# A decoder layer on one core: its mixers' second half earlier, operands in halves, and low parts of weights on another engine

## The chip, the cores and the metric

The kernel runs on one core of one Trainium2 chip. The metric is the device time of one execution in microseconds (us), the median of several runs. Engines are named as in the profile: PE (TensorE, matrix products), DVE (VectorE), ACT (ScalarE), POOL (GpSimd) and SP (SyncE, which issues most transfers).

## What is computed

One layer on 1024 positions of width 1024, all in float32. Two token mixers in parallel (a causal gMLP in 8 groups with chunks of 128, and a latent attention of 16 heads), then cross-attention into 256 memory tokens, then a mixture of experts: 8 groups of 8 experts, the best group, two experts in it, each of width 256.

```python
def hybrid_layer(x, mem, positions, ...):
    proj = x @ w_in + b_in
    u, v, c_q, c_kv, k_rope_raw, gate_gm, gate_mla = jnp.split(proj, IN_SPLITS, axis=-1)
    y_gm = gmlp_branch(gelu(u), gelu(v), gm_ln_g, gm_ln_b, gm_w_s, gm_b_s) @ w_gm_out
    y_mla = mla_branch(c_q, c_kv, k_rope_raw, positions, ...) @ w_mla_out
    merged = sigmoid(gate_gm) * y_gm + sigmoid(gate_mla) * y_mla
    x = layer_norm(DEEPNORM_ALPHA * x + merged @ w_o, ln1_g, ln1_b)
    x = layer_norm(DEEPNORM_ALPHA * x + memory_cross_attention(x, mem, ...), ln2_g, ln2_b)
    y_moe = hierarchical_moe(x, ...)
    return layer_norm(DEEPNORM_ALPHA * x + y_moe, ln3_g, ln3_b)
```

The gMLP branch is `u * (tril(w_s) @ layer_norm(v) + b_s)` by chunks and groups; an expert is `(silu(x @ w_gate) * (x @ w_up)) @ w_down`.

## The kernel before

Every float32 product is made of three: each operand is split into a rounded high part (ACT copies it into the type float32r) and a low part (the difference, a subtraction, mostly on DVE), and `mm3` (L123) adds high by high, high by low and low by high. `split` (L108) makes both parts, `load_w` (L114) loads a weight tile and splits it. Raw weight tiles have three buffers, split ones five, so loads and splits run several projections ahead of PE.

The dense stages (all up to the router) aren't ordered by hand: a planner orders the instructions of each engine and the issues of SP by its own model of time, keeping data and buffer dependencies. From the router on, in `manual_schedule` regions, PE, ACT, DVE and POOL run in the order in which the program emits them (the first `turn_x` of the experts lies between two such regions); SP's issues are still the planner's.

The stages in order:

- `latents` (L220): x is loaded transposed in 8 tiles of 512 KB (`xraw`) with a weight tile (`w_cq`) for every two, split, and multiplied as it comes. `late_consts` (L205) then makes the router's constants and loads six small ones (`b_t`, `g_q`, `g_kv`, `b_s`, `rope_c`, `b_r`); the first reader is the scaling of the latent (L264).
- `mla_proj`, `proj_v`: queries, keys and values of the attention go to DRAM; so does v of the gMLP.
- Gates and gMLP: `proj_in_t` (L311) makes one block of 128 columns, 48 products of 512 columns. Projections 8 to 23 alternate with the 8 steps `st` of each half of `gmlp` (L674). The call `gmlp(half)` loads four v tiles, normalizes and splits them into `vs` (one buffer), and each step writes its block of the result to `a_d` in DRAM.
- `load_a` (L737) loads `a_d` back in 8 tiles of 512 KB (`aT`) and splits them. Then come the last projection from `xT`, the pools of the attention (`mla_pools`; they reuse the memory of `xT`) and `gate_gm` (L744), whose 8 projections alternate with steps of `mla`: the first step loads q, k and v of head 0 (`load`, L478), the second runs the first product with them (L506).
- `mla`: attention by hand, in one list. The sums of the softmax go to DRAM and come back as `fac` in a chain of small transfers issued by POOL (`factors`, L762).
- `mem_kv` (L634): key projections f = 0 to 7 of the memory (24 products of 256 columns each), then value projections. Between them `scale_o` (L789) scales the attention output, one block a step: two products of `fac` with a selection (L798), then DVE.
- `merge`, `out_ln`, `mem_attn`, `out_ln`, then the router.
- The experts: 32 pairs. Each pair has six weight tiles of 1 MB (four of gate and up, two of down); tile m is `raw`, then `high(m)` on ACT (`wh`), then `low` (`wl`, L1435). `ahead` in `experts` (L1447) prepares one tile ahead at each of six points of a pair; `low(m)` also issues the load of tile m + 11 or m + 12. Tiles with m % 6 == 5 (`slow`) get their low part on POOL, the others on DVE. `turn_x` (L1312) transposes a pair's gathered rows and splits them, `hidden` (L1335) applies Silu and the mask, `store` (L1390) adds up the output.
- Before the first pair, `router_masks` (L1162) sums the masks on PE and DVE, `warm` (L1155) puts products without a reader on PE, and tiles 0 to 2 get their parts: the low parts of 0 and 1 on DVE, that of 2 on POOL.
- `final_loads` (L1557) spreads the last norm's two vectors over 128 partitions with products in full float32, in pairs 20 to 24; `final` (L1573) adds, normalizes and stores 8 row tiles.

## Time and profile before

| | us |
|---|---|
| median of 3 runs | 2033.64 (2032.84 to 2034.22) |
| profiled execution | 2035.97 |
| its span, first to last instruction | 2034.2 |
| PE busy | 1977.6 (97%) |
| DVE busy | 1292.5 (64%) |
| ACT busy | 1003.3 (49%) |
| POOL busy | 449.2 (22%) |

[...] The page's 40 slices show PE at nine tenths or more in all but three: the first, the one around 1400 and the last. How to read it: PE is the engine with the least idle time, so another engine's time matters only where PE waits for it.

### The profile page before, as it was taken

To read this page: it belongs to the slowest core of one execution; us is meant where nothing else is said; L and a number is where in the kernel's file an instruction comes from. 1 tells how busy PE (TensorE), PEld (TensorE's weight loads), DVE (VectorE), ACT (ScalarE), POOL (GpSimd) and SP (SyncE) were. 2 spreads that over 40 slices of the span, in tenths; PEclk is the share of its full clock that TensorE was granted. 3 is DMA by queue.
4 is the path that set the end of the run, shared out by engine and by line. 5 is a ranking of instruction groups with operands and counts; after the bars stand their busy time and mean duration, and the time that the engine had idled before them with its cause. 6 is when DMAs were issued, how large, how long until landed. Compare 5 with 4: busy or idle time off the path is not lost.

```text
span 2034.2 us, 25602 instructions
## 1 busy us (share of the span) xinstructions
PE 1977.6 (97%) x9468; PEld 1630.4 (80%) x9468; DVE 1292.5 (64%) x2040; ACT 1003.3 (49%) x1267; POOL 449.2 (22%) x243
## 2 busy tenths in 40 slices
PE   8999999999999999999999999997999999999996
PEld 8888888888787777777888888886788888888884
DVE  5636533441335888857436516477888888888887
ACT  4432422322304777764212315233777777777774
POOL 0002000000100111110001100022545555557752
PEclk9999999999999999999999999997999999999998
DMA  5154963353783555537535712555899999999966
GB/s 184 54 210 155 382 196 134 143 189 136 245 251 104 126 125 125 125 133 239 184 106 180 268 62 73 161 218 231 286 372 381 381 387 396 401 392 369 377 260 250
DMA packets 147897, 457.29 MB, mean 225 GB/s; under 512 B 18077, under 2 KB 64029, under 8 KB 118744
## 3 DMA queue, kind: packets, MB, share of 16 engines
q1 hardware_dynamic: 138040, 438.58, 61.7%
q0 software_dynamic: 9728, 17.03, 2.2%
q8 instruction: 76, 1.25, 0.2%
q14 instruction: 53, 0.43, 0.1%
HBM read 367.10 MB, written 104.79 MB: 232 GB/s over the span
## 4 chain that ended last, share of the span: by engine, by line
PE 91%; DMA 3%; DVE 3%; ACT 1%; issue 1%; SPq 0%; POOL 0%; POOLq 0%; ACTq 0%
PE bank L125 9%; PE bank L126 9%; PE bank L127 9%; PE py L1355 8%; PE bank L380 8%; PE bank L382 8%; PE bank L384 8%; PE pg L125 6%; PE pg L127 5%; PE pg L126 5%; PE po L564 2%; PE po L566 2%; PE po L565 2%; PE st L538 1%; PE st L540 1%; PE st L542 1%
## 5 line engine op out<-in xcount | busy, mean ns | idle before, releaser
L1426 ACT ACTIVATE wh<-raw 128x2048 fp32r<-128x2048 f32 (+1 forms) x198 | 361.1, 1859 | 36.3 <-issue 31.4
L1435 DVE TENSOR_TENSOR wl<-raw,wh 128x2048 fp32r<-128x2048 f32 (+1 forms) x166 | 363.3, 2236 | 4.6 <-PE pg L126 3.0
L1435 POOL TENSOR_TENSOR wl<-raw,wh 128x2048 fp32r<-128x2048 f32 x32 | 202.9, 6340 | 227.6 <-ACT wh L1426 227.6
L110 ACT ACTIVATE wsp<-wraw 128x1024 fp32r<-128x1024 f32 (+5 forms) x118 | 111.6, 947 | 263.7 <-PE bank L384 155.2
L125 PE MATMUL pg<-wh,ex 128*128 128x512 f32 x512 | 203.4, 397 | 0.7 <-ACT ex L110 0.7
L126 PE MATMUL pg<-wl,ex 128*128 128x512 f32 x512 | 200.0, 391 | 2.0 <-DVE wl L1435 2.0
L127 PE MATMUL pg<-wh,ex 128*128 128x512 f32 x512 | 200.6, 392 | 0.0
L111 DVE TENSOR_TENSOR wsp<-wraw,wsp 128x1024 fp32r<-128x1024 f32 (+5 forms) x118 | 127.6, 1083 | 96.2 <-ACT wsp L110 93.7
L1355 PE MATMUL py<-wh,ehs 128*128 128x512 f32 x512 | 143.7, 402 | 2.9 <-DVE ehs L111 2.4
L380 PE MATMUL bank<-xT,wsp 128*128 128x512 f32 x384 | 120.1, 390 | 0.0
L382 PE MATMUL bank<-xT,wsp 128*128 128x512 f32 x384 | 119.9, 390 | 0.0
L384 PE MATMUL bank<-xT,wsp 128*128 128x512 f32 x384 | 119.7, 390 | 0.0
L735 POOL TENSOR_TENSOR xr<-xr,lb 128x1024 f32<-128x1024 f32 x12 | 28.7, 2395 | 409.4 <-ACT xr L734 409.4
L546 ACT ACTIVATE pe<-st 128x768 f32<-128x768 f32 (+5 forms) x128 | 86.3, 674 | 59.6 <-DVE st L544 59.5
L126 PEld LDWEIGHTS pg<-wl,ex 128*128 128x128 f32 x512 | 96.7, 189 | 21.3 <-DVE wl L1435 2.3
L125 PEld LDWEIGHTS pg<-wh,ex 128*128 128x128 f32 x512 | 96.4, 188 | 21.1 <-ACT lgb L1571 1.5
L127 PEld LDWEIGHTS pg<-wh,ex 128*128 128x128 f32 x512 | 96.5, 189 | 20.6
L1355 PEld LDWEIGHTS py<-wh,ehs 128*128 128x128 f32 x512 | 91.3, 189 | 19.4 <-DVE ehs L111 3.1
L125 PE MATMUL bank<-wsp,xT 128*128 128x512 f32 (+2 forms) x256 | 91.2, 363 | 6.5 <-ACT wsp L110 6.5
L319 ACT ACTIVATE to<-bank,cols 128x512 f32<-128x512 f32 x48 | 30.4, 684 | 133.7 <-PE bank L384 133.7
L548 ACT ACTIVATE pq<-pe 128x768 fp32r<-128x768 f32 (+5 forms) x128 | 91.3, 713 | 4.1
L126 PE MATMUL bank<-wsp,xT 128*128 128x512 f32 (+2 forms) x256 | 91.6, 358 | 0.0
(410 smaller groups left out, 4627.4 us busy)
## 6 DMA issues: line engine op xcount, KB each, us to landing
raw<-w_gu SPq DMA_DIRECT2D x124, 1024.0 KB
raw<-w_dn SPq DMA_DIRECT2D x62, 1024.0 KB
wraw<-w_t SPq DMA_DIRECT2D x24, 512.0 KB
kn_d<-st SPq DMA_DIRECT2D x8, 1024.0 KB
qn_d<-st SPq DMA_DIRECT2D x8, 1024.0 KB
vv_d<-vt SPq DMA_DIRECT2D x16, 512.0 KB
qT<-qn_d SPq DMA_DIRECT2D x16, 512.0 KB
kT<-kn_d SPq DMA_DIRECT2D x16, 512.0 KB
```

What stands on the lines that cost most here:

```text
L110: a = nc.scalar.activation(hi, src, AF.Copy)
L111: (lo_eng or nc.vector).tensor_tensor(lo, src, hi.bitcast(F32), op=ALU.subtract)
L125: mm(out, ah, bh, start=start, stop=False)
L126: mm(out, ah, bl, start=False, stop=False)
L127: mm(out, al, bh, start=False, stop=stop)
L380: mm(ps, wh, x.at(0, kt, h), start=st, stop=False)
L382: mm(ps, wh, x.at(1, kt, h), start=False, stop=False)
L384: mm(ps, wl, x.at(0, kt, h), start=False, stop=sp)
L548: nc.scalar.activation(pq[:, 0, q0:], e[:, q0:], AF.Copy)
L1355: self.nc.tensor.matmul(py[:, q * 512:(q + 1) * 512], hs[:, a, js], w[b][:, j * 1024 + q * 512:j * 1024 + (q + 1) * 512], start=start and ...
L1426: self.nc.scalar.activation(w[0][:, c], self.raws[n][:, c], AF.Copy)
L1435: eng.tensor_tensor(w[1][:, c], self.raws[n][:, c], w[0][:, c].bitcast(F32), op=ALU.subtract)
```

## The change

- Start: the first x tile and the first weight tile are loaded and split in two halves each, alternating, x first. The six small constants are issued by POOL instead of SP, each made to wait for the rounding of the last x tile.
- Mixers: `gmlp(1)` stands before projection 15 instead of after it, its steps go with projections 17 to 20 instead of 18 to 21, and `load_a` has two projections (22, 23) behind it instead of one.
- `mem_kv`: the first step of `scale_o` that stands between key projections comes after f = 6 instead of f = 5.
- Experts: the low part of tile 0 goes to DVE between the two halves of the mask products, that of tile 1 after the masks, then the first pair's rows are transposed and split, then the low part of tile 2, on DVE instead of POOL. A Silu of one column stands behind the `warm` products on ACT. Tile 5's low part is DVE's too (`slow` from m = 11 on).
- Final vectors: four row halves, each loaded, split into high and low and spread by two float32r products, one half every two pairs from 20 to 28, instead of float32 products on whole rows.
- Tail: the last row tile's last operation and its store are done in halves.

```diff
--- before.py
+++ after.py
@@ -202,10 +202,12 @@
         self.ones = p.tile([128, 128], FR, name="ones")
         ts(self.ones, jp, 0.0, 1.0, op0=ALU.mult, op1=ALU.add)
 
-    def late_consts(self):
+    def late_consts(self, behind):
+
         self.router_consts()
         for t, n in ((self.bt, "b_t"), (self.gq, "g_q"), (self.gkv, "g_kv"), (self.bs, "b_s"), (self.fr, "rope_c"), (self.rb, "b_r")):
-            self.nc.sync.dma_start(t, self.i[n])
+            d = self.nc.gpsimd.dma_start(t, self.i[n])
+            self.tc.add_manual_dep(d.ins, behind.ins.name, mybir.DependencyInfo(mybir.DependencyClass.Sync, mybir.DependencyReason.DATA), reason="behind larger transfers")
 
     def natural(self, ps, t, x, w, kts=range(8), nk=8):
 
@@ -227,8 +229,20 @@
             for kk in range(4):
                 for kt in (2 * kk, 2 * kk + 1):
                     raw = self.gp.tile([128, 1024], F32, name="xraw", tag="g")
+                    if kt == 0:
+
+                        wraw = self.rawp.tile([128, 1024], F32, name="wraw", tag="wraw")
+                        wt = self.wp.tile([128, 2, 1024], FR, name="wsp", tag="wsp")
+                        cs = [(slice(512 * j, 512 * j + 512), slice(384 * j, 384 * j + 384)) for j in range(2)]
+                        for c, cw in cs:
+                            nc.sync.dma_start(raw[:, c], self.i["xT"][kt][:, c])
+                            nc.sync.dma_start(wraw[:, cw], self.i["w_cq"][kk][:, cw])
+                        for c, cw in cs:
+                            self.split(xT.at(0, kt, c), xT.at(1, kt, c), raw[:, c])
+                            self.split(wt[:, 0, cw], wt[:, 1, cw], wraw[:, cw])
+                        continue
                     nc.sync.dma_start(raw, self.i["xT"][kt])
-                    self.split(xT.at(0, kt, ALL), xT.at(1, kt, ALL), raw)
+                    self.last = self.split(xT.at(0, kt, ALL), xT.at(1, kt, ALL), raw)
                     if kt % 2 == 0:
                         wt = self.load_w(self.i["w_cq"][kk], 768)
                 for kt in (2 * kk, 2 * kk + 1):
@@ -236,7 +250,7 @@
                     for t in range(8):
                         self.natural(pss[t][:, :384], t, xT, lambda k: (wt[:, 0, o:o + 384], wt[:, 1, o:o + 384]), [kt])
                     self.unit()
-            self.late_consts()
+            self.late_consts(self.last)
             bcq = small.tile([128, 384], F32, name="bcq", bufs=1)
             self.bcast(bcq, self.i["b_cq"])
             bkv = small.tile([128, 320], F32, name="bkv", bufs=1)
@@ -654,7 +668,7 @@
             self.load_o(f)
             if f == 0:
                 next(fac, None)
-            if f in (5, 7):
+            if f in (6, 7):
                 next(scale)
         for sl in range(2):
             wts = [self.load_w(self.i["w_mv"][sl, kk], 1024) for kk in range(4)]
@@ -1444,11 +1458,10 @@
         gi = self.main[0]
         return {i: self.gather(i, gi[:, i:i + 1]) for i in range(3)}
 
-    def experts(self, rest, xg):
+    def experts(self, rest, xg, x):
         nc, tc = self.nc, self.tc
         gi, si, al = self.main
-        xs = {}
-        xs[0] = self.turn_x(xg[0], 2)
+        xs = {0: x}
         mask = self.main_mask
         ready = 0
         order = contextlib.ExitStack()
@@ -1457,7 +1470,7 @@
         for i in range(NP):
             def ahead():
                 nonlocal ready
-                slow = lambda m: m % 6 == 5 and m < 6 * NP - 6
+                slow = lambda m: m % 6 == 5 and 6 < m < 6 * NP - 6
                 m = ready + 2
                 self.high(m + 1)
                 if slow(m + 1):
@@ -1491,7 +1504,7 @@
                 sel = self.select(gi[:, NP - 1:])
             if i == 24:
                 self.nb = nc.values_load(self.nbi[0:1, 0:1], min_val=0, max_val=15)
-            if i in (22, 24):
+            if 21 <= i <= 28:
                 next(lgb, None)
             if i == NP - 1:
                 self.flush()
@@ -1558,16 +1571,18 @@
         nc = self.nc
         self.lgb = px.enter_context(self.pool("lgb", side="right")).tile([128, 2, 1024], F32, name="lgb")
         self.fin = px.enter_context(self.pool("fins", 8, side="right"))
-        one = self.fin.tile([1, 128], F32, name="one", bufs=1)
-        nc.gpsimd.memset(one, 1.0)
         for j, n in enumerate(("ln3_g", "ln3_b")):
-            row = self.fin.tile([1, 1024], F32, name="row", bufs=1)
-            nc.sync.dma_start(row, self.i[n])
-            yield
             for q in range(2):
                 c = slice(q * 512, (q + 1) * 512)
+                high, low = (self.fin.tile([1, 512], FR, name=m, bufs=1) for m in ("high", "low"))
+                row = self.lgb[:1, j, c]
+                nc.sync.dma_start(row, self.i[n][:, c])
+                yield
+                self.split(high, low, row)
+                yield
                 pg = self.bank_g()
-                nc.tensor.matmul(pg, one, row[:, c], start=True, stop=True)
+                nc.tensor.matmul(pg, self.ones[:1], high, start=True, stop=False)
+                nc.tensor.matmul(pg, self.ones[:1], low, start=False, stop=True)
                 nc.scalar.activation(self.lgb[:, j, c], pg, AF.Copy)
 
     def final(self, first=True):
@@ -1620,8 +1635,12 @@
                 nc.scalar.activation(u, u, AF.Copy, scale=r)
                 nc.gpsimd.tensor_tensor(u, u, lb, op=ALU.add)
             else:
-                stt(u, u, r, lb, op0=ALU.mult, op1=ALU.add)
-            nc.sync.dma_start(self.out[t], u)
+                for c in halves if t == 7 else [slice(0, 1024)]:
+                    stt(u[:, c], u[:, c], r, lb[:, c], op0=ALU.mult, op1=ALU.add)
+                    if t == 7:
+                        nc.sync.dma_start(self.out[t][:, c], u[:, c])
+            if t < 7:
+                nc.sync.dma_start(self.out[t], u)
 
         rows = [row_sum(t) for t in range(8)]
         for t in range(9):
@@ -1707,20 +1726,20 @@
                             st(2 * j)
                             k.proj_in_t(xT, 11 + j)
                             st(2 * j + 1)
+                        st = k.gmlp(1)
                         k.proj_in_t(xT, 15)
-                        st = k.gmlp(1)
                         k.proj_in_t(xT, 16)
-                        k.proj_in_t(xT, 17)
                         for j in range(4):
                             st(2 * j)
-                            k.proj_in_t(xT, 18 + j)
+                            k.proj_in_t(xT, 17 + j)
                             st(2 * j + 1)
-                        k.proj_in_t(xT, 22)
+                        k.proj_in_t(xT, 21)
                         k.flush()
-                    w = k.load_w(k.i["w_t"][23], 1024)
+                    w = k.load_w(k.i["w_t"][22], 1024)
                     aT = Act(front.enter_context(k.pool("aT", 8, side="right")), "aT")
                     k.load_a(aT)
-                    k.proj_in_t(xT, 23, w)
+                    k.proj_in_t(xT, 22, w)
+                    k.proj_in_t(xT, 23)
                     k.flush()
                 k.mem_load(late)
                 k.mla_pools(mla)
@@ -1796,15 +1815,17 @@
                 wts.remove(q)
     m = k.router_masks()
     next(m)
+    k.low(0, nc.vector)
     k.warm(6)
     next(m, None)
     k.warm(16)
+    nc.scalar.activation(k.rp.tile([128, 1], F32, name="silu"), k.i128[:, :1], AF.Silu)
     k.high(2)
-    for n in range(2):
-        k.low(n, nc.vector)
-    k.low(2, nc.gpsimd)
+    k.low(1, nc.vector)
+    x = k.turn_x(xg[0], 2)
+    k.low(2, nc.vector)
     order.close()
-    k.experts(rest, xg)
+    k.experts(rest, xg, x)
     return k
 
 
```

## Rows read from the trace of the kernel before

**Rows 1.** Page, part 1: engine, busy us (share of the span), instructions.
```profile
PE 1977.6 (97%) x9468; PEld 1630.4 (80%) x9468; DVE 1292.5 (64%) x2040; ACT 1003.3 (49%) x1267; POOL 449.2 (22%) x243
```

**Rows 2.** Timeline, start: start, us, engine line operation tiles [idle before, releaser].
```profile
6.53 2.93 PE L125 MATMUL bank<-wsp,xT 128*128 128x384 f32 x8 [6.53 <-ACT wsp L110]
...
6.89 1.06 ACT L110 ACTIVATE xT<-xraw 128x1024 fp32r<-128x1024 f32 x1 [0.41 <-DMA xraw<-xT]
...
22.87 1.06 ACT L110 ACTIVATE xT<-xraw 128x1024 fp32r<-128x1024 f32 x1 [0.29 <-DMA xraw<-xT]
...
50.02 1.84 ACT L264 ACTIVATE cqT<-bank,cols 128x512 fp32r<-128x512 f32 x3 [3.12 <-PE bank L262]
```

**Rows 3.** Chain that ended last, its first piece: start, us, what.
```profile
0.77 3.89 DMA xraw<-xT
```

**Rows 4.** Timeline, end of the mixers: SP's issues, then PE.
```profile
529.17 3.83 SPq L741 DMA_DIRECT2D aT<-a_d  x8
...
541.17 0.47 SPq L489 DMA_DIRECT2D kT<-kn_d  x1
...
552.98 0.76 PE L506 MATMUL bank<-kT,qT 96*128 96x256 f32 x2 [4.41 <-DMA kT<-kn_d]
...
553.55 1.05 PE L380 MATMUL bank<-aT,wsp 128*128 128x512 f32 x2
...
558.37 0.62 PE L380 MATMUL bank<-aT,wsp 128*128 128x512 f32 x2
```

**Rows 5.** Chain that ended last: down products, final vectors' products.
```profile
1792.11 4.11 PE py L1355 x18
...
1813.95 1.91 PE pg L1570 x4
```

**Rows 6.** Waits of PE, whole span: us in total, times, longest.
```profile
PE py L1355 <- DVE ehs L111: 2.4, 1, 2.4
...
PE bank L382 <- DVE aT L111: 0.6, 1, 0.6
```

**Rows 7.** Timeline, scaling of the attention output, PE.
```profile
919.77 1.21 PE L798 MATMUL bank<-fac,fsel 32*128 32x512 f32 x2 [2.26 <-DMA fac<-rinv_d]
```

**Rows 8.** Stretches: us, PE PEld DVE ACT POOL busy, PEclk, DMA, GB/s.
```profile
910.00:915.00 5.00, 5.00 (x44) 5.00 (x43) 2.74 (x4) 1.28 (x3) 0.52 (x1) 1.00 1.02 374
...
920.00:925.00 5.00, 5.00 (x21) 4.35 (x22) 3.56 (x5) 1.46 (x2) 0.00 (x0) 0.50 0.93 299
```

**Rows 9.** Timeline, pairs 2 and 5: low parts on DVE and POOL.
```profile
1464.22 6.34 DVE L1435 TENSOR_TENSOR wl<-raw,wh 128x2048 fp32r<-128x2048 f32 x1
...
1519.97 2.28 DVE L1435 TENSOR_TENSOR wl<-raw,wh 128x2048 fp32r<-128x2048 f32 x1
...
1520.30 6.44 POOL L1435 TENSOR_TENSOR wl<-raw,wh 128x2048 fp32r<-128x2048 f32 x1 [7.79 <-ACT wh L1426]
```

**Rows 10.** Timeline, start of the experts: POOL, DVE, PE, ACT.
```profile
1408.24 4.56 POOL L1435 TENSOR_TENSOR wl<-raw,wh 128x2048 fp32r<-128x2048 f32 x1 [0.22 <-ACT wh L1426]
...
1408.49 0.23 DVE L1170 COPY pws<-pov 128x64 f32<-128x64 f32 x1 [1.81 <-PE pov L1168]
...
1408.75 4.09 DVE L1171 TENSOR_TENSOR pws<-pws 128x32 f32<-128x32 f32 x1
...
1411.61 0.60 PE L1317 MATMUL px<-ident,xg 128*128 128x128 f32 x4
...
1418.20 1.11 PE L1317 MATMUL px<-ident,xg 128*128 128x128 f32 x4 [2.01 <-DVE ex L111]
...
1424.75 1.28 ACT L1339 ACT_TABLE_LOAD   x1
...
1430.99 1.03 PE L1317 MATMUL px<-ident,xg 128*128 128x128 f32 x8
```

**Rows 11.** Waits of DVE, 1800 to 1960: us in total, times, longest.
```profile
DVE eh L1340 <- ACT eh L1339: 16.2, 12, 1.5
```

**Rows 12.** Chain that ended last, its last piece.
```profile
2027.71 1.29 DVE raw L1623
```


## The prediction, on record before the changed kernel was run

> **What bounds the kernel now.** I read the busy table of the page first: PE is busy for 97% of the span [rows 1]. So only three things can move the time: time in which PE waits, time in which it runs at the lower of its two clocks, and products that it need not do. The second view was the list of what PE waited for, and the third the table by stretches, read for the granted clock. The span holds 56.6 us in which PE isn't busy, and nearly all of them lie in a handful of places: the start, the end of the mixers, the scaling of the attention output, the start of the experts, and the tail. From pair 3 of the experts on, PE waits for nothing until the last pair. The fourth view was the timeline around each place, engine by engine, to see which instruction came last there. Each part of the change goes to one of these places, so I price them one by one and add.
>
> **The start.** PE's first product comes at 6.53 [rows 2]. Ahead of it in one chain stand the landing of the first x tile (512 KB, 3.89 us from issue) [rows 3], its rounding on ACT (1.06, as that of the next tile [rows 2]) and that of the weights (the rest, 6.53 - 4.66 - 1.06 = 0.8). Now x and weights come in halves, x half first. The next x tile is rounded from 6.89 on, after a wait for its landing [rows 2]; so 384 KB of weights and 512 KB of x landed in the 2.2 us since 4.66, or 0.41 MB per us. A half tile of 256 KB is then there some 0.6 us before the whole, at about 4.05 (estimate). Half a rounding of x is about 0.6, half of one of weights about 0.5 (both estimates a little over the half, for an instruction's start): first product at 5.2, a gain of 1.3. PE isn't starved behind it, since the products of one x tile take it longer than the next tile's landing. Bounds: 1.6, and a loss of 0.3 if the halves land one behind the other rather than together. [...]
>
> The six small constants leave SP's queue for POOL's and wait there for the rounding of the last x tile, which ended at 23.9 in the trace [rows 2]. POOL has nothing queued behind them until the projections of the attention. Their first reader is the scaling of the latent at 50.02 [rows 2], so there are 26 us for six small transfers: nothing gained, nothing lost. If that cover were gone, the loss would be what they come late.
>
> **The mixers.** The second half of the gMLP stands one projection earlier, and two projections, not one, stand between the loads of its result (aT) and its first use. In the trace SP issues the eight aT loads (4 MB) from 529.17 on; one projection later the tiles of head 0 reuse xT's memory, and kT is issued at 541.17 behind them. It lands 11.7 us later, and PE waits 4.41 for it [rows 4]. What follows runs slow: the two products with kT and twelve of the next projection take from 552.98 to 558.37 [rows 4], 5.4 us, where twelve at 0.228 each [rows 5] and two half as wide take 3.0: 2.4 lost. PE also waited 0.6 for aT's low part [rows 6]. Sum 7.4. With two projections (some 22 us) behind the load, aT's 4 MB are through (10 us at 0.41 MB per us) before head 0 is issued. Ahead of kT then stand about 2 MB, 5 us and a latency, against the 11 us of the projection that hides it (48 products at 0.228): the wait goes, and nothing is late next. Moved with it: the setup of the second half (four v tiles, DVE and ACT work) must be ready one projection sooner; it has the same two projections of cover as the first half has, for which PE didn't wait. Bounds 0 and 7.6; I take 7.4.
>
> **The scaling.** One step of it moves behind the seventh key projection instead of the sixth. PE waited 2.26 for fac [rows 7]; in the next 5 us it did 21 products at a granted clock of 0.50, against 44 in 5 us before it at 1.00 [rows 8]. Two of the 21 are twice as wide, so they count as 23, or 2.6 us at full clock: 2.4 lost. The key projection that now stands in between has 24 products, 2.7 us at 44 in 5 us, which covers the 2.26 with 0.5 to spare. Gain 2.26 + 2.4 = 4.7; bounds 0 (fac later by as much as it is hidden) and 5.0.
>
> **The start of the experts.** Three low parts (2.28 us each [rows 9]) matter here. The third ran on POOL from 1408.24; DVE's add of 32 columns for the masks, issued at 1408.75, took 4.09 [rows 10]. The same happens at 1464.22, a low part of 6.34 on DVE [rows 9]. So an operation on DVE with two operands in SBUF waits while POOL's runs. Behind the add stood both other low parts and the low half of x, so PE's second four transposes came at 1418.20, although the first four ran at 1411.61 [rows 10]. Now the first low part fills DVE's wait of 1.81 ahead of the copy of the masks [rows 10], so the copy comes 0.45 later, the add costs 0.2 and not 4.09, the second low part ends at about 1412.0, the low half of the first half of x (after its rounding on ACT) at 1413.5, and the transposes follow to 1414.1 (if they again wait for that half). The 48 products of the pair at 0.228 [rows 5] and 0.2 of turning the hidden rows end at 1425.3, against 1430.99 [rows 10]: 5.7. The table load of 1.28 for Silu, in the trace after the first products [rows 10], falls into ACT's idle time before. Taken off again: the third and sixth low part are now DVE's. Six low parts are 13.7 us; with some 4.4 us of small work DVE has 18.1 in a pair that takes PE 17.7. I take off 0.7: 5.0. Bounds: 1 (DVE gives the rest back in the next two pairs) and 6. The wait of 2.4 in the third pair [rows 6] I leave as it is.
>
> **The final vectors.** Four products of full float take 1.91 us, twice [rows 5]; they become eight rounded ones at 0.228, 1.8 in all. Gain 3.8 - 1.8 = 2.0; bounds 0 and 2.5. The four new splits (some 0.6 each on ACT and DVE) stand at the head of four pairs; DVE waits up to 1.5 for ACT before the gate of a pair (16.2 in 12 waits [rows 11]), which covers them. Their rows are four small loads on SP, each a whole pair ahead of its split.
>
> **The tail.** The last multiply-add takes 1.29 and ends the work [rows 12]; the store of 512 KB follows. In halves, the second store is 256 KB: 0.6 less at 0.41 MB per us, the first being under way. Bounds -0.3 and 0.8. [...]
>
> **Sum.** 1.3 + 7.4 + 4.7 + 5.0 + 2.0 + 0.6 = 21.0. The profiled execution took 2035.97 and would take 2015.0. It lay 2.33 above the median of the runs, 2033.64, which becomes 2012.6. The median is what I predict.
>
> **The rivals.** (a) The plan of the first stages isn't fixed by hand, so the new order may leave a wait where kT's was: head 0's loads still wait for xT's memory, and only 3 us are spare. Then most of the 7.4 stays, say 5.5: 2018. For it speaks that kT took 11.7; against it that the 4 MB ahead of it are gone. (b) DVE becomes the bound in the first pairs, and 4.5 of the 5.0 come back as waits for low parts: 2017. For it speaks the wait of 2.4 in pair 2, behind a DVE that was late; against it that DVE has some 2.6 us to spare in each later pair. (c) fac is again late, its chain of small transfers being slowed by others: 2017.3. (d) Slower: POOL keeps every sixth low part from the second pair on. In the steady pairs DVE's low part starts only 0.33 before POOL's (1519.97 against 1520.30) [rows 9]. If DVE comes later by more than that, it is POOL that starts first, DVE is held 4.1 (6.34 less 2.28 [rows 9]), and PE waits 2.4 [rows 6]. Lost in all 30 pairs, that is 72, less the one already there: 2082. The work that the change puts on DVE pushes this way. [...] Against it speaks that the trace lost the order once, in pair 2, and had it back from pair 3 on: PE's wait gives DVE the time. (e) The change doesn't do what it says, because the planner puts loads and steps where they were: then only the last three parts are left, and where DVE gives those back as well, 2031.
>
> **How the numbers follow.** Forecast, all six parts within their small errors: 0.52, with a range of its own of 2009 to 2016. (a) 0.13, (b) 0.14, (c) 0.07, two of these together (2021 to 2023) 0.06, (e) 0.04, (d) 0.04. The likeliest is the forecast, 2012.6. The range runs from 2009 (the upper bounds of the parts add up to 2.5, and pair 2 may lose half its wait) to 2021, which takes in (a), (b) and (c) alone, and leaves out 0.14 with the pairs of rivals, (d) and (e). About 0.2%, 4 us, is what a measurement of this kernel can tell from no change. Faster by more: 0.92; within: 0.04, which is (e); slower: 0.04, which is (d).
>
> **What would show it.** Right: PE's first product near 5.2; no wait for kT and none for fac, and a granted clock of 1.00 in both stretches; the masks' add at 0.2 us, and the second four transposes of x before 1415 on the old clock; eight short products for the vectors. Wrong: a new wait of more than 2 us in PE's list, above all one for a low part in the first three pairs, or DVE low parts above 6 us in more than one pair.

## The result: 17.5 us faster, 3.9 behind the forecast

| | before | after |
|---|---|---|
| median | 2033.93 (4 runs, 2032.84 to 2035.64) | 2016.47 (4 runs, 2015.20 to 2018.18) |
| ratio | | 0.9914, 95% interval 0.9897 to 0.9931 |
| profiled execution | 2035.97 | 2016.14 |
| its span | 2034.2 | 2014.4 |

The forecast was 2012.6 with a range of 2009 to 2021. The time lies inside it, on the slow side. PE does the same number of products and waits less; its busy time falls too (against [rows 1]), mostly because products at the lower clock count as busy for longer (in [rows 8], 21, two of them of double width, fill 5.00 us at 0.50 and 44 at 1.00; the clock records of both traces hold only these two values) and fewer of them run at it (mean granted clock 0.989 against 0.985). First part 1 of the page of the changed kernel, then its list of what PE waited for (us in total, times, longest), cut to the lines that answer to [rows 4, 6, 7] and one new one:

```profile
PE 1969.8 (98%) x9468; PEld 1624.5 (81%) x9468; DVE 1293.0 (64%) x2049; ACT 1006.0 (50%) x1274; POOL 462.1 (23%) x246
```
```profile
PE py L1369 <- DVE ehs L111: 2.4, 1, 2.4
PE pm L520 <- DMA kT<-kn_d: 1.9, 5, 0.6
...
PE bank L520 <- issue: 1.4, 1, 1.4
```

The wait for fac is gone, that for aT too. The 2.4 for ehs in the third pair is still there, as said. Of the 4.41 for kT a wait of 1.4 is left at the same product, with no releaser named.

Where the time went shows best as a **lead**: the start of the same product in both traces, before minus after.

| product | before | after | lead | gained since the line above | forecast |
|---|---|---|---|---|---|
| first of all | 6.53 | 4.95 | 1.58 | 1.6 | 1.3 |
| first with cqT | 163.80 | 161.53 | 2.27 | 0.7 | 0 |
| first with kT | 552.98 | 546.75 | 6.23 | 4.0 | mixers, |
| last with aT | 634.95 | 626.36 | 8.59 | 2.4 | 7.4 together |
| first key projection of the memory | 897.83 | 889.46 | 8.37 | -0.2 | 0 |
| last with fac | 955.86 | 941.62 | 14.24 | 5.9 | 4.7 |
| first transposes of the experts | 1411.61 | 1397.82 | 13.79 | -0.4 | 0 |
| transposes in the first pair, for the second | 1430.99 | 1411.12 | 19.87 | 6.1 | experts' start, |
| the same for the fifth | 1487.99 | 1469.74 | 18.25 | -1.6 | 5.0 together |
| the same for the last | 1971.08 | 1952.05 | 19.03 | 0.8 | 2.0 |
| end of the span | 2034.2 | 2014.4 | 19.8 | 0.8 | 0.6 |

The parts gave 19.8 where 21.0 was forecast. The places themselves, in the timeline of the changed kernel (start, us, engine line operation tiles) and in the tables by stretch (us, PE PEld DVE ACT POOL busy, PEclk, DMA share, GB/s).

**Start**, answering to [rows 2, 3]. Timeline of the changed kernel; then stretches of the kernel before, from 6 and 12, and of the changed one, from 5 and 9:

```profile
4.95 1.65 PE L125 MATMUL bank<-wsp,xT 128*128 128x384 f32 x4 [4.95 <-ACT wsp L110]
6.39 0.52 PE L126 MATMUL bank<-wsp,xT 128*128 128x384 f32 x1
6.71 0.52 PE L127 MATMUL bank<-wsp,xT 128*128 128x384 f32 x1
```
```profile
6.00:10.00 4.00, 3.47 (x11) 3.47 (x12) 3.87 (x4) 3.33 (x4) 0.00 (x0) 1.00 1.02 405
12.00:16.00 4.00, 4.00 (x25) 4.00 (x24) 2.85 (x3) 1.35 (x3) 0.24 (x1) 1.00 0.63 172
```
```profile
5.00:9.00 4.00, 4.00 (x13) 4.00 (x14) 1.83 (x4) 1.11 (x2) 0.00 (x0) 1.00 0.80 303
9.00:13.00 4.00, 4.00 (x25) 4.00 (x24) 2.86 (x3) 3.40 (x4) 0.00 (x0) 1.00 1.03 415
```

The first products of the program start 0.32 apart, later ones 0.17. In 4 us PE does 11 (in the 3.47 that were left) or 13 of them, and then 25: half the rate, though PEclk shows 1.00, so it is the spacing that has to be read here. (The first clock record of the trace lies at 11.9 before and at 8.8 now, just where the spacing changes; ahead of it the table counts 1.00 for want of a record.) The slow beginning lasted from 6.53 to 11.82 before, 16 products, and from 4.95 to 8.88 now, 12 products. That difference isn't the halves' doing: in the eleven kernels below that start in the same way it is 9 to 19 products. From the first product to the 31st it takes 7.1 here, 6.7 to 8.1 in those eleven, and 7.7 in the kernel before.

**Mixers and scaling**, answering to [rows 4, 7, 8]. Changed kernel: SP's issues and PE's first product with kT, the stretch behind that and the one in front of it, and the first product with fac, which has no wait now; last, a stretch of the kernel before that follows the second one of [rows 8]:

```profile
515.99 4.28 SPq L755 DMA_DIRECT2D aT<-a_d  x8
...
537.27 1.16 SPq L503 DMA_DIRECT2D kT<-kn_d  x1
...
546.75 0.48 PE L520 MATMUL bank<-kT,qT 96*128 96x256 f32 x2 [1.36 <-issue]
```
```profile
540.00:547.00 7.00, 5.64 (x26) 4.41 (x25) 1.29 (x2) 1.06 (x1) 0.00 (x0) 1.00 1.09 263
547.00:552.00 5.00, 5.00 (x24) 4.16 (x24) 1.85 (x6) 0.00 (x0) 0.00 (x0) 1.00 1.07 310
```
```profile
911.40 0.73 PE L812 MATMUL bank<-fac,fsel 32*128 32x512 f32 x2
```
```profile
925.00:930.00 5.00, 5.00 (x33) 4.51 (x32) 1.97 (x4) 1.82 (x4) 0.00 (x0) 0.84 0.23 89
```

Behind the 1.36 at 546.75 the clock stays at 1.00 (24 products in 5 us), so the low stretch of the kernel before is gone. The 1.36 itself isn't fixed: at the same product the eleven kernels below with the new order of the mixers have 0.2 to 2.95. In the kernel before, the low clock behind the wait for fac went on past 925: 0.84 in the mean of the next 5 us.

**Start of the experts**, answering to [rows 10]: DVE, then PE:

```profile
1392.59 2.29 DVE L1449 TENSOR_TENSOR wl<-raw,wh 128x2048 fp32r<-128x2048 f32 x1
1394.79 0.22 DVE L1184 COPY pws<-pov 128x64 f32<-128x64 f32 x1
1395.05 0.19 DVE L1185 TENSOR_TENSOR pws<-pws 128x32 f32<-128x32 f32 x1
...
1397.82 0.70 PE L1331 MATMUL px<-ident,xg 128*128 128x128 f32 x4
...
1399.92 0.66 PE L1331 MATMUL px<-ident,xg 128*128 128x128 f32 x4
...
1411.12 1.03 PE L1331 MATMUL px<-ident,xg 128*128 128x128 f32 x8
```

The masks' add takes 0.19, not 4.09, and the second four transposes come 2.1 behind the first four, not 6.6. Of the 6.1 gained up to the second pair, 4.0 are two waits of PE (2.01 each, at 1415.4 and 1418.2 in the kernel before) that are gone. The rest is about what the low clock behind the first of them cost: 0.50 in the mean of the 5 us from 1415.4, where the changed kernel has 1.00.

**Third pair**, answering to [rows 9]: the low part on DVE and the one on POOL of the changed kernel, and the stretch behind PE's wait; then two stretches of the kernel before, at and behind the same wait:

```profile
1444.35 6.34 DVE L1449 TENSOR_TENSOR wl<-raw,wh 128x2048 fp32r<-128x2048 f32 x1
...
1443.93 4.61 POOL L1449 TENSOR_TENSOR wl<-raw,wh 128x2048 fp32r<-128x2048 f32 x1 [7.72 <-ACT wh L1440]
```
```profile
1452.00:1457.00 5.00, 5.00 (x18) 3.91 (x17) 4.60 (x4) 3.98 (x3) 0.90 (x1) 0.66 0.90 351
```
```profile
1468.00:1473.00 5.00, 2.58 (x13) 1.79 (x12) 4.59 (x5) 1.62 (x3) 4.30 (x3) 1.00 0.52 164
1473.00:1478.00 5.00, 5.00 (x24) 3.88 (x23) 5.00 (x4) 5.00 (x3) 0.00 (x0) 1.00 1.03 397
```

POOL starts 0.42 ahead of DVE, and DVE is held, as before: 6.34 for a low part that takes 2.28 elsewhere, ending 2.15 after POOL's. But now the granted clock falls behind the wait (0.66 in the mean of 5 us, 18 products for 24), which it didn't before.

**Final vectors and tail**, answering to [rows 5, 12]: PE in one of the four pairs, and the last piece of the chain:

```profile
1795.09 0.61 PE L1369 MATMUL py<-wl,ehs 128*128 128x512 f32 x2
1795.64 0.49 PE L1584 MATMUL pg<-high,ones 1*128 1x512 f32 x1
1795.97 0.38 PE L1585 MATMUL pg<-low,ones 1*128 1x512 f32 x1
1796.29 0.50 PE L125 MATMUL pg<-wh,ex 128*128 128x512 f32 x1
1796.62 0.40 PE L126 MATMUL pg<-wl,ex 128*128 128x512 f32 x1
```
```profile
2009.35 0.75 DVE raw L1639
```

### The profile page after: what moved, and what is told of

Read it like the earlier page. It is cut to its first block, busy times and chain, and to the rows that moved or that the text cites. A ratio compares the mean times of both kernels' runs of the same rounds, so it can differ in the third digit from the quotient of the medians.

```text
span 2014.4 us, 25629 instructions
## 1 busy us (share of the span) xinstructions
PE 1969.8 (98%) x9468; PEld 1624.5 (81%) x9468; DVE 1293.0 (64%) x2049; ACT 1006.0 (50%) x1274; POOL 462.1 (23%) x246
## 4 chain that ended last, share of the span: by engine, by line
PE 92%; DVE 3%; DMA 2%; issue 1%; ACT 1%; SPq 0%; POOL 0%; DVEq 0%; POOLq 0%; ACTq 0%
PE bank L125 9%; PE bank L126 9%; PE bank L127 9%; PE py L1369 9%; PE bank L394 8%; PE bank L396 8%; PE bank L398 8%; PE pg L125 6%; PE pg L127 6%; PE pg L126 6%; DMA kT<-kn_d 2%; PE po L578 2%; PE po L580 1%; PE po L579 1%; PE px L1331 1%; PE st L554 1%
## 5 line engine op out<-in xcount | busy, mean ns | idle before, releaser
L1449 POOL TENSOR_TENSOR wl<-raw,wh 128x2048 fp32r<-128x2048 f32 x30 | 192.8, 6427 | 215.5 <-ACT wh L1440 215.5
```

Source lines behind the costliest of these rows:

```text
L1449: eng.tensor_tensor(w[1][:, c], self.raws[n][:, c], w[0][:, c].bitcast(F32), op=ALU.subtract)
```

## The experiments

Leads and losses are against the profiled execution of the changed kernel, and medians against its 2016.47. One thing has to be known for all of them. In nine of these kernels (the changed one among them) the order of the instructions of PE and of SP is the same up to the experts. Still their first key projection of the memory starts anywhere from 889.46 to 894.65, the changed kernel's being the earliest; its waits for kT in the attention come to 1.9, those of low2_pool to 5.0. In counts_late, the latest, the wait in front of the first product with kT is 2.95, with the clock at 0.50 behind it. So whole times differ by a few us for no reason of the edit, and where the edit lies in the experts, the stretch from their first transposes to the end is the better measure. It is 616.6 in the changed kernel.

| kernel | median (runs) | ratio to before, 95% interval | that stretch |
|---|---|---|---|
| u_start | 2019.67 (4) | 0.9920, 0.9902 to 0.9939 | |
| u_mixers | 2022.60 (4) | 0.9924, 0.9906 to 0.9943 | |
| u_scaling | 2022.40 (4) | 0.9932, 0.9914 to 0.9951 | |
| u_experts | 2021.46 (4) | 0.9924, 0.9908 to 0.9941 | 621.8 |
| counts_late | 2016.55 (4) | 0.9904, 0.9887 to 0.9921 | 618.5 |
| vectors_dma | 2014.17 (4) | 0.9895, 0.9878 to 0.9912 | 613.0 |
| both | 2014.09 (4) | 0.9891, 0.9873 to 0.9909 | 613.1 |
| mix_slack | 2024.99 (4) | 0.9948, 0.9931 to 0.9965 | |
| best | 2014.45 (5) | 0.9897, 0.9882 to 0.9912 | 613.3 |
| low2_pool | 2017.40 (1) | | 616.5 |
| low0_behind | 2017.10 (1) | | 616.9 |
| spread | 2008.09 (4) | 0.9864, 0.9847 to 0.9880 | 608.6 |

### Undoing one part each

**u_start**: the branch for the first tile taken out.

```diff
-                    if kt == 0:
-                        ...
-                        continue
                     nc.sync.dma_start(raw, self.i["xT"][kt])
```

> The changed kernel with the first x tile and weight tile loaded and split whole again; the six small constants stay on POOL. Theory (the halves alone made the start's gain): PE's first product goes from 4.95 back to 6.5, and the end of the first transposes' wait goes from 47.28 back to 49.6, all 2.3 of the lead that the traces show there; time 2016.5 + 2.3 = 2018.8. Rival (the constants' way off SP's queue made the 0.7 beyond the first product's 1.6): first product 6.5, but the transposes at 48.9; time 2018.1.

First product at 6.14; PE's slow beginning, with products 0.32 apart, until 11.7. 1.9 are lost by the first use of cqT (161.53 to 163.47) and 2.1 by the first product with kT, where the kernel before has lost 2.3 by the first use of cqT. Of the 1.9, 1.2 are the later first product, which is what the halves do. The other 0.7 is a slow beginning of 17 products instead of 12, and its length differs between kernels that start alike (9 to 19). What the constants' way did is at most 0.3 to 0.4, no more than the first product differs here from the kernel before. The median, 3.2 behind, lies beyond both expectations, as whole times here may.

**u_mixers**: `gmlp(1)`, its steps and `load_a` in the old places. List of PE's waits, and a stretch:

```diff
-                        st = k.gmlp(1)
                         k.proj_in_t(xT, 15)
+                        st = k.gmlp(1)
...
-                    k.proj_in_t(xT, 22, w)
-                    k.proj_in_t(xT, 23)
+                    k.proj_in_t(xT, 23, w)
```

> The changed kernel with the mixers in the old order: the second gMLP call after projection 15, one projection behind the loads of aT. Theory: PE waits some 4.4 for kT of head 0 again, runs at a granted clock of 0.50 for some 5 us behind it, and the wait of 1.4 that the changed kernel has there is gone; 6.3 lost, 2022.8, and the small waits for kT in the attention fall from 1.9 in all to 0.6. Rival (the order isn't what moved the time; head 0's loads wait for the memory of xT in either order): the wait for kT stays near 1.4, the clock stays at 1.00, and the time within 1.5 of 2016.5.

```profile
PE bank L520 <- issue: 5.6, 1, 5.6
```
```profile
553.72:558.72 5.00, 5.00 (x16) 4.14 (x17) 0.71 (x5) 0.00 (x0) 0.00 (x0) 0.66 1.08 277
```

The wait is 5.6 and the clock behind it low again, 0.66 in the mean of 5 us; the lead over the kernel before shrinks by 8.5 up to the last product with aT, 1.0 of it ahead of the mixers. The old order has 4.41 and 5.57 at this product, the twelve kernels with the new one 0.2 to 2.95, so the order did move the time, through the wait and the clock that the prediction named. The new order doesn't rule such a wait out, though. In counts_late, an experiment below whose mixers are in the new order, the product and the 5 us behind it read:

```profile
547.93 0.77 PE L520 MATMUL bank<-kT,qT 96*128 96x256 f32 x2 [2.95 <-issue]
```
```profile
547.93:552.93 5.00, 5.00 (x13) 4.04 (x14) 1.85 (x6) 0.00 (x0) 0.00 (x0) 0.50 1.07 241
```

The side remark was wrong: the waits for kT in the attention didn't fall but were 3.8.

**u_scaling**: one number back. PE at the product with fac, and the stretch behind it:

```diff
-            if f in (6, 7):
+            if f in (5, 7):
```

> The changed kernel with the first scaling step between key projections after f = 5 again. Theory by the prediction's step: PE waits about 2.3 for fac and then runs at a granted clock of 0.50; 4.7 lost, 2021.2. By the traces' lead, which grew by 5.9 across this stage: 2022.4. Rival (fac comes earlier in the changed kernel for another reason, so that the sixth place would do as well): no wait for fac and 2016.5.

```profile
912.65 0.73 PE L812 MATMUL bank<-fac,fsel 32*128 32x512 f32 x2 [2.58 <-DMA fac<-rinv_d]
```
```profile
913.00:918.00 5.00, 5.00 (x41) 4.69 (x40) 3.53 (x4) 1.54 (x2) 0.00 (x0) 1.00 0.83 261
```

The wait is back, at 2.58, but in this execution the clock stayed at 1.00 behind it. The profiled one took 2018.16, the other three 2020.76, 2024.03 and 2024.54. So the projection that was put in between hides 2.3 to 2.6 for certain, and a low clock that not every execution has. That the slower runs are those with the low clock would fit, and the mean granted clock of the two slowest is 0.988 against 0.990 in the other two; but they have no trace that shows where.

**u_experts**: order and engines of the low parts as before, no early table load. POOL, then DVE:

```diff
-    k.low(0, nc.vector)
     k.warm(6)
     next(m, None)
     k.warm(16)
-    ...
     k.high(2)
-    k.low(1, nc.vector)
-    x = k.turn_x(xg[0], 2)
-    k.low(2, nc.vector)
+    for n in range(2):
+        k.low(n, nc.vector)
+    k.low(2, nc.gpsimd)
```

> The changed kernel with the start of the experts as it was: both first low parts on DVE behind the masks, the third and sixth low part on POOL, no early table load. Theory: the masks' add takes 4.1 again and the second transposes are 5.9 later, but the wait of 2.4 in the third pair isn't followed by a low clock, as in the kernel before, so that 1.7 of it comes back: 4.2 lost, 2020.7. Rival (the low clock behind that wait doesn't depend on the start of the experts): the clock is lower there too, 5.9 lost, 2022.4.

```profile
1394.17 4.56 POOL L1449 TENSOR_TENSOR wl<-raw,wh 128x2048 fp32r<-128x2048 f32 x1 [0.24 <-ACT wh L1440]
...
1394.67 4.11 DVE L1185 TENSOR_TENSOR pws<-pws 128x32 f32<-128x32 f32 x1
```

6.9 are lost by the second pair's transposes and 1.6 come back in the third pair, where the wait of 2.4 is followed by a clock of 1.00, as in the kernel before. The theory held in both halves, 5.2 in all.

### What frees the masks' add

**low2_pool** and **low0_behind** undo one half of that part each: the third low part on POOL ahead of the transposes, or the first low part behind the masks.

```diff
 # low2_pool
     k.low(1, nc.vector)
+    k.low(2, nc.gpsimd)
     x = k.turn_x(xg[0], 2)
-    k.low(2, nc.vector)
 # low0_behind
-    k.low(0, nc.vector)
     k.warm(6)
 ...
+    k.low(0, nc.vector)
     k.low(1, nc.vector)
```

> The changed kernel with the third low part back on POOL, ahead of the first transposes; everything else as changed. Theory (an operation on DVE with two operands in SBUF waits while POOL's low part runs, and DVE's operations that read PSUM too if they share SBUF): POOL's low part starts behind ACT's high part at about 1397.5 and runs 4.5; the first half of x's low part (128x512, 0.69 at 1399.18) ends only at about 1402.4 and PE's first gate product waits 2 to 3 longer. Rival (that operation has one operand in PSUM and isn't held): it takes 0.69 as before, and PE loses nothing.

> The changed kernel with the first low part behind the masks again, as in the kernel before, but still nothing on POOL. Theory (freeing the masks' add from POOL made most of the gain, filling DVE's wait the smaller part): the add takes 0.2, the first low part starts about 0.5 later than the masks' copy, both low parts end 1.9 later than in the changed kernel, and the second pair's transposes come 1.9 later. Rival (the gain is the order on DVE): they come 4 or more later.

POOL (two rows) and DVE (two rows) of low2_pool, then POOL of low0_behind:

```profile
1394.67 2.73 POOL L1314 DMA_INDIRECT xg<-x_d,xgi  x1 [0.30 <-issue]
...
1400.28 4.62 POOL L1449 TENSOR_TENSOR wl<-raw,wh 128x2048 fp32r<-128x2048 f32 x1
...
1394.25 2.28 DVE L1449 TENSOR_TENSOR wl<-raw,wh 128x2048 fp32r<-128x2048 f32 x1
...
1400.44 0.69 DVE L111 TENSOR_TENSOR ex<-px,ex 128x512 fp32r<-128x512 f32 x1 [1.05 <-ACT ex L110]
```
```profile
1393.65 0.99 POOL L1314 DMA_INDIRECT xg<-x_d,xgi  x1 [0.30 <-issue]
```

Up to the second pair's transposes low2_pool loses nothing and low0_behind 0.4 (PE waits 0.39 for the low half of x), where both together (u_experts) lose 6.9. For low0_behind I had expected 1.9: the freed add did make most of the gain, and the order on DVE still less than I thought. My theory for low2_pool fell and its rival held: the subtraction at 1400.44, which reads one operand from PSUM, takes 0.69 in the middle of POOL's low part, and PE loses nothing. That the masks' add, too, was free there has its reason in POOL's gathers. With the first low part on DVE at 1394.25, the gather issued at 1394.67 takes 2.73 instead of 0.99, the next one 2.56, and POOL comes to its low part only at 1400.28, long after the masks' add (1396.70). So either edit alone keeps POOL out of the add's way; the move of the third low part to DVE wasn't needed beside the first.

### The race in the third pair

**counts_late**, **both** and **best** move the router's counts (five small operations on DVE, 0.93 together), the last two with the vectors spread by transfers (**vectors_dma**):

```diff
 # counts_late, both
-            if i == 1:
+            if i == 3:
                 over = self.router_counts()
...
-            if i >= 1:
+            if i >= 3:
                 next(over, None)
 # best: next(over, None) in first(), in the middle of a pair
 # vectors_dma, both, best, spread
-                high, low = (self.fin.tile([1, 512], FR, name=m, bufs=1) for m in ("high", "low"))
-                ...
+                self.bcast(self.lgb[:, j, c], self.i[n][:, c])
+                yield
```

> The changed kernel with the router's counts begun two pairs later, so that their five small operations on DVE (0.93 together) don't stand ahead of the third pair's last low parts. Theory (DVE and POOL race there, and DVE loses by less than 0.93): DVE's low part starts before POOL's in the third pair and takes 2.28 instead of 6.34, PE's wait of 2.4 for ehs and the low clock behind it are gone, 4.1 gained: span 2010.3, 2012.4. Rival (DVE is behind by its six low parts anyway, the counts are not what decides): the wait of 2.4 comes in the same pair or the next one, 2016.5.

DVE, then POOL, two pairs later:

```profile
1485.67 6.35 DVE L1449 TENSOR_TENSOR wl<-raw,wh 128x2048 fp32r<-128x2048 f32 x1
...
1485.26 4.61 POOL L1449 TENSOR_TENSOR wl<-raw,wh 128x2048 fp32r<-128x2048 f32 x1 [7.73 <-ACT wh L1440]
```

The third pair has no wait; the wait of 2.4, with the low clock behind it, stands where the counts now are. They decided the race in both places, so nothing is gained: the mechanism held, the gain didn't. (The stretch is 1.9 longer because the clock, low at its beginning in all kernels, rose later: 0.60 in the mean of the 5 us from 1403.4.)

> The changed kernel with the four halves of the final vectors spread over the 128 partitions by transfers (256 KB each) instead of splits and products. Theory: the four pairs that took 18.60 in the changed kernel take 17.73 like the others, 3.5 gained, 2013.0. Rival (the transfers share the DMA engines with the weights, 0.92 to 0.99 busy in this stage; 1 MB more is 2.6 at 0.39 MB per us): weight tiles come late, PE waits for a raw tile's parts in the last ten pairs, and 2.6 of the 3.5 are given back: 2015.6.

The four pairs take 17.73 like the rest; 3.5 are gained between the transposes that the changed kernel has at 1788.96 and those of the last pair, and PE waits for no weight. The rival fell: 1 MB more, in a stage whose DMA engines are 0.92 busy, cost nothing here.

> The changed kernel with both edits, counts two pairs later and vectors spread by transfers. Theory: the two gains add, 4.1 + 3.5: span 2006.8, 2008.9. If both rivals hold: 2015.6.

The two edits didn't add: the wait came back two pairs later, as in counts_late, and 3.5 is all that is left.

> The changed kernel with two edits: the vectors spread by transfers, and the counts' steps moved from the head of a pair to its middle, behind the low part that races with POOL's, where DVE waits 1.49 for the next gate anyway. Theory (the counts decide the race wherever they stand ahead of it; behind it they cost nothing): no wait for ehs in any pair from the second on, no low clock after 1400; 2.4 + 1.7 there and 3.5 for the vectors: span 2006.8 give or take the 1 to 3 by which the attention differs from one execution to the next; 2009. Rival (DVE is behind by its own low parts in the first pairs, and loses the race in one of them without the counts too): one wait of 2.4 stays, 2013.

DVE, then POOL, in the third pair:

```profile
1447.61 4.35 DVE L1199 TENSOR_SCALAR past<-i,cn 32x8 f32<-32x8 f32 x1
...
1445.50 6.43 POOL L1449 TENSOR_TENSOR wl<-raw,wh 128x2048 fp32r<-128x2048 f32 x1 [7.72 <-ACT wh L1440]
```

Here DVE's low part came first and took 2.28, but the second operation of the counts, on 32 rows of 8, took 4.35: it waited for the end of POOL's. PE then waited 2.7 for ehs. Neither expectation had this mechanism; the rival's one wait and 2013 came near for another reason.

**spread** gives one of the seven operations to a pair:

```diff
         yield
         v.tensor_scalar(cn, pc[:NP, 0:1], -1024.0, None, op0=ALU.add)
+        yield
         v.tensor_scalar(past, self.i8[:NP], 128.0, cn, op0=ALU.mult, op1=ALU.is_lt)
+        yield
         v.tensor_reduce(out=ob, in_=past, op=ALU.add, axis=AX.X)
 ...
```

> The changed kernel with the vectors spread by transfers and the counts' seven small operations on DVE given one to a pair, at its head, from the fourth pair on. The reading that is tested: DVE reaches the low part that races with POOL's 0.15 after it could (a wait for ACT's gate) and starts 0.27 ahead of POOL, so 0.42 in all may stand ahead of it; one operation of 0.14 to 0.22 fits, all five (0.93) or the last two (0.37) with a little delay don't. If so: no wait for ehs behind a low part of 6.3 in any pair, no low clock after 1400, 4.1 gained there beside 3.5 for the vectors: from the first transposes of the experts to the end 7.6 less than in the changed kernel; the median 2016.5 - 7.6 = 2009. Rival (DVE's backlog from its six low parts loses the race in some pair anyway): one wait of 2.4 stays and that stretch is 3.5 shorter; 2013.

DVE in the fifth pair (the first operation of the counts, the racing low part), POOL's low part, and all of PE's waits of more than 0.2 from 1415 to 1990:

```profile
1473.37 0.14 DVE L1198 TENSOR_SCALAR cn<-pov 32x1 f32<-32x1 f32 x1
...
1479.60 2.28 DVE L1454 TENSOR_TENSOR wl<-raw,wh 128x2048 fp32r<-128x2048 f32 x1
...
1479.87 6.49 POOL L1454 TENSOR_TENSOR wl<-raw,wh 128x2048 fp32r<-128x2048 f32 x1 [7.73 <-ACT wh L1445]
```
```profile
PE py L1374 <- ACT ehs L110: 0.5, 1, 0.5
PE pf L1616 <- DVE raw L1623: 0.5, 2, 0.2
```

DVE starts 0.27 ahead, no pair waits for a low part, and the stretch is 8.0 shorter, 3.5 of it by the vectors. With 2008.09 this kernel is faster than both: 0.9864 of the one before, with an interval that lies below the changed kernel's.

### An attempt at more room for the loads of head 0

**mix_slack**: meant to run the first product of the attention one gate projection later.

```diff
-            for _ in range((2, 2, 2, 2, 2, 2, 1, 0)[f]):
+            for _ in range((1, 2, 2, 2, 2, 2, 2, 0)[f]):
```

> The changed kernel with the first product of the attention one gate projection later (11 us more between the loads of head 0 and its first use). Theory (the wait of 1.36 at 545.39 that no releaser is named for is still head 0's loads, late by SP's issue and the small rows of the rope parts): the wait is gone, 1.4 gained, 2015.1. Rival (the wait belongs to the switch from the projection to the attention, not to the loads): it moves one projection later and stays 1.4, 2016.5.

```profile
546.29 0.36 PE L520 MATMUL bank<-kT,qT 96*128 96x256 f32 x1 [0.65 <-issue]
...
595.87 0.27 PE L536 MATMUL bank<-ident,mx 128*8 128x128 f32 x1 [3.36 <-DVE mx L531]
```

The edit doesn't do what the expectation says. The first step of `mla` loads head 0 and the second runs the first product; with one step behind the first projection instead of two, that second step stays where it was (546.29, x1 instead of x2), and only the steps behind it come a projection later. So the wait in front of it, 0.65 here, says nothing on the 1.36: it lies within the 0.2 to 2.95 of the kernels in which nothing was moved. Whether the 1.36 is head 0's loads stays an argument from the kernel before, where the same product waits for kT. What the edit did is a new wait of 3.36 for a later step of the attention, which with the low clock behind it cost 5.1. The 2.0 that the attention lost besides are within what kernels of one order differ by. In the experts the race is lost twice, in the third pair and again in the fifth, where the last two operations of the counts (0.37) stand and DVE had waited 0.31 more: 4.3 more. It ends 8.5 behind the changed kernel.

The tail, the early table load, and the vectors' products against those of the kernel before weren't undone alone; their sizes are those of the traces.

## Why the prediction was near, and where its steps were off

- **Start** (1.3, measured 2.3). First product at 4.95, near the 5.2: 1.6 gained. The other 0.7 is PE's slow beginning, 12 products 0.32 apart instead of 16. It stood in [rows 2], with eight products in 2.93, and I read them as ordinary. That it was shorter isn't an effect of the change (9 to 19 products in other kernels with the same start): this 0.7 is luck.
- **Mixers** (7.4, measured 6.3). The low clock (2.4) and the wait for aT (0.6) went as sized. The step that failed is "the wait goes, and nothing is late next": kT was to need 5 and a latency, and it was used 9.5 after its issue, which itself came 2.7 after the first load of head 0. In that stretch the DMA engines were busy all the time, at 263 GB/s and not at my 0.41 MB per us. 1.4 stayed, a third of the 4.41, most likely by the mechanism of rival (a): head 0's first load was issued at 534.54, just as the last projection from xT had ended. In other kernels of this order it is 0.2 to 2.95, so neither the 1.4 nor the clock that held behind it is certain.
- **Scaling** (4.7, measured 5.9). The order and the hidden wait were right. The term that was mis-sized is the low clock: I counted 5 us of it, up to 925, and it went on; the row behind has 0.84, which is 0.8 more.
- **Start of the experts** (5.0, measured 6.1 - 1.6 = 4.5). The 4.09 of the add and its freedom were right. That DVE's extra low parts would cost 0.7 was wrong in kind: they cost nothing there, but the third pair kept its wait of 2.4, "as it is", and got a low clock behind it. I had priced the wait and not the clock. DVE's own low parts, the reason of rival (b), didn't make that wait; the counts did, since spread has the same low parts and no wait.
- **Final vectors** (2.0, measured 0.8). The term "eight at 0.228" was mis-sized. Two products of one row come 0.33 and 0.32 after each other, with 0.09 ahead and 0.10 more for the product behind them: about 0.87 a pair, 3.5 in four, against 4.3 in two before (18.60 and 19.87 for a pair of 17.73).
- **Tail** (0.6, measured 0.8): right in sign and nearly in size. The two halves of the last store move without a gap between them (DMA share 1.00 from 2010.5 to 2011.0 and 1.03 from there to 2011.5), and from the end of the last operation to the end of the span it takes 4.3, against 5.2 with the whole store. At the start the first half of x landed 3.05 after its issue, against 3.89 for the whole; the second landed only 5.09 after its own, at 6.80, with the DMA share at 0.34 from 5 to 6, but PE had products all the while.
- **The median.** The profiled execution lay 2.33 above the median of three, and I carried that over. In the 34 executions of the kernel before that these comparisons hold, the median is 2034.9 (2032.14 to 2040.75): the profiled one was 1.1 above it, and against that median the changed kernel is 18.4 faster rather than 17.5. The changed kernel's was 0.3 below its median. Of the 3.9 that the forecast missed, 1.2 are the parts, 2.3 that offset, 0.3 the rest.
- **Rival (d)** stayed away in the steady pairs, but its mechanism is real (6.34 and 6.35 for a low part that POOL's was ahead of, 2.28 for one ahead of POOL's) and the margin as thin as read: 0.93 ahead of DVE's low part lost the race in both places tried, 0.37 lost it in mix_slack, behind a wait of 0.31, and not in the changed kernel, 0.14 to 0.22 never. It doesn't last: PE's wait gives DVE its time back (one wait of 2.4 for ehs in the whole span, before as after).

## What to carry to other kernels

Price a wait together with the low clock that may follow it, and read that clock to the row where it is back at 1.00. Where two engines hold each other up, look for the small operation that makes one of them late, and spread it rather than move it. Take the offset between a profile and the median from many runs, and compare leads at named products rather than whole times when a few us differ by themselves. Before a lead is put down to an edit, look at the same place in other kernels that leave it alone. And read in the order of products of a new kernel whether the edit moved what it was to move.

## What the runs showed of the hardware

- POOL's gathers are held by DVE too: 0.99 in low0_behind, 2.73 and 2.56 in low2_pool (2.74 and 2.55 in the changed kernel), each of the longer ones ending 0.86 to 0.87 after a low part on DVE that was running at its start. Which part of a gather is held isn't shown.
- On DVE, beside a running low part on POOL, three operations were seen to be held: the low part (6.34 for 2.28), the masks' add with both operands in SBUF (4.09 for 0.19) and the second operation of the counts, on 32 rows of 8 (4.35 in best, 0.22 in the changed kernel). The subtraction with one operand in PSUM was not (0.69 at 1400.44 in low2_pool, 0.69 in the changed kernel with POOL idle). What divides them beyond these cases isn't shown.
- The clock after a wait isn't settled by the wait. Behind the 2.4 in the experts it fell in eleven of the thirteen profiled executions that had this wait; the two in which it stayed at 1.00 are those with the old start of the experts (the kernel before, u_experts). Behind 2.26 for fac it fell, behind 2.58 it didn't. At the first product with kT it fell behind 2.95, 4.41 and 5.57 and stayed behind 0.2 to 1.5. What decides stays open.
